# Low-rank latents: squares, sums and roots among the last projection panels, scaling and splitting in single steps beside neighbourhood heads

## The chip, the core and the metric

The kernel runs on one core of one Trainium2 chip. The metric is the device time of one execution, in microseconds (us), as the median of the runs shown. A core has TensorE (PE in the profile, with its weight loads as PEld), VectorE (DVE), ScalarE (ACT), GpSimd (POOL) and the DMA queue of SyncE (SP); each works through its own instructions in order, and semaphores hold an instruction until what it reads is there and what it overwrites has been read.

## What is computed

Two layers of a transformer over 512 latent tokens (on a grid 64 wide) and 256 context tokens, model width 1024. The first layer has two groups of heads, 8 heads of neighbourhood attention and 8 heads of multi-head latent attention (MLA), then SwiGLU; the second has sliding-window attention and SwiGLU. The change is in the MLA part of the first layer. There the input projection gives each token a query latent of 256 numbers and a key/value latent of 128, and each is normalised before it is used:

```python
def rms_norm(x, gain=None):
    y = xf * lax.rsqrt(jnp.mean(xf * xf, axis=-1, keepdims=True) + EPS)
    return y * gain
...
q = rms_norm(p[..., :MLA_Q_RANK], q_norm) @ w_q_up
c_kv = rms_norm(p[..., MLA_Q_RANK:MLA_Q_RANK + MLA_KV_RANK], kv_norm)
```

So each latent needs its squares, their sum over the features, a root with its reciprocal, and a multiplication by that factor and by the gain.

## The kernel before, in words

Activations lie with features on the 128 partitions and tokens along the free axis: 512 latent tokens (LATS), then 256 context tokens (CTXS). A product in full precision is three products of high and low parts: `mm3` issues wh x high (L335), wh x low (L337) and wl x high (L338) for each of 8 blocks of the contraction. High parts are ACT casts (L324 for weights, L361 in `split` for activations), low parts are differences on DVE (L325, L362).

The first layer begins with the modulated input (16 tiles) and then the loop `projections` (L1003): 12 panels of 128 weight columns, one after the other, each first for LATS and then for CTXS, each into a PSUM bank from a ring of seven (`PG`, L126). First come queries and keys of head pairs 0 and 1, then the panels that the string `AFTER` names in turn: 0, 1 and 2 are the query latent's two tiles and the key/value latent (tiles `lat_raw`, written by ACT at L738), k is the rotary key (rotated by ACT L464, DVE L465 and POOL L467 to L469), and 5 to 8 are queries and keys of head pairs 2 and 3. After each quarter of a panel the loop yields, and a share `DBG` of a modulation step is made beside it (`bg`). A modulation tile there is two halves of 512 columns: DVE multiplies and sums for one of the two condition vectors (L255, shown as ISA in the order and as CUSTOM_DVE in the profile, with L259 at the end), POOL multiplies in place for the other (L272), ACT sums (L273), DVE adds up (L275, L276).

Then come the neighbourhood heads, in pairs 0 to 3 (`na_jobs`, L1135). Each pair is three jobs: scores on PE (L745, L746) into three PSUM banks, a maximum on DVE that also frees the bank (`take`, L555), the exponential on ACT (L551), transposes on PE (L499) into banks that DVE (L490) or ACT (L491) copies out, products with the values (L545), at the end a factor for each query (L475 to L482). Beside each job `attend` lets a queue of side work advance by as many steps as `STEPS` says for that pair; a step is what a generator does up to its next yield. `ORDER` says what joins the queue at which pair: splitting of the raw queries and keys of pair 2 at pair 0, the latents' norms (n) and pair 3's splitting at pair 1, the preparation of the MLA heads (m) at pair 2.

The norms are `gained` (L968), called from `latent_norms` (L1050), in three steps. The first squares the three latent tiles on POOL (L978), adds the two squares of the query latent on DVE (L982), sums over the features on PE (L985: for each 128 tokens a product of the squares with one column of ones; twelve of them, in one bank), takes two roots on ACT (L988, behind a load of ACT's table for it) and the reciprocal on DVE (L989). The second and the third do one group each: for LATS and for CTXS PE spreads the factors over a bank (`spread`, L367; banks of the pair `PQ`, which the transposes of the heads use as well), DVE scales in place (L965), and ACT and DVE split into high and low parts (L361, L362).

The order in which instructions stand on each engine is decided by a scheduler that goes by the priorities of the program's text and by its own estimate of when each could run; it is fixed before the kernel runs.

Of the kernel before, what the change touches and what calls it, by code (L numbers as in the profile page):

```python
# [11 lines left out]
AF = mybir.ActivationFunctionType  # L12
ALU = mybir.AluOpType
# [39 lines left out]
OUTQ = 1  # L53
E1, EF = 1, 1
ORDER = ("2", "n3", "m", "")
AFTER = "012k5678"
DBG = 0.38
KC = (0, 1, 0)
VP = 0
TURN1, MANY = (0,), 0  # L60
# [8 lines left out]
PATTERN = ("fbsfbsfbbsfs",) * 3  # L69
BG = ((0, 0, 0, 0, 0), (2, 3), (0, 0), (0, 0))  # L70
FIRST = 2000
STEPS = ((2, 3, 4, 4), 5, 3)
HALVES = (slice(0, 256), slice(256, 512))
SWAP8 = [(i // 16) * 16 + (i % 16 + 8) % 16 for i in range(32)]
SWAP16 = [(i + 16) % 32 for i in range(32)]
# [23 lines left out]
def hybrid_kernel(ctx: ExitStack, tc, I, out):  # L99
# [17 lines left out]
    def B(dt=F32, tag="b"):  # L117
        return T(tag, [P, NT], dt)
# [226 lines left out]
    def PQ():  # L345
        return PS("d")
# [389 lines left out]
    def put(t, rows=P, scale=1.0):  # L736
        def use(src, c):
            marks["put"] = S.activation(t[:rows, c], src, AF.Copy, scale=scale)  # L738

        return use  # L740
# [216 lines left out]
    def gain(tiles, g0, col):  # L957

        for c in (LATS, CTXS):
            d, n = PQ(), c.stop - c.start  # L960
            for i in range(n // P):
                at = c.start // P + i
                spread(d[:, i * P : (i + 1) * P], col[:, at : at + 1].to_broadcast([P, P]))
            for j, t in enumerate(tiles):
                V.scalar_tensor_tensor(t[:, c], t[:, c], gains[:, g0 + j : g0 + j + 1], d[:, :n], op0=ALU.mult, op1=ALU.mult)  # L965
        return tiles

    def gained(groups):  # L968

        d, m = PQ(), NT // P  # L970
        n = m * len(groups)
        col = T("sm", [P, 6, 2]).rearrange("p a b -> p (a b)")[:, :n]
        for i, (tiles, _) in enumerate(groups):
            acc = None
            for t in tiles:
                s = B()
                if SQ:
                    G.tensor_tensor(s, t, t, op=ALU.mult)  # L978
                else:
                    S.activation(s, t, AF.Square)  # L980
                if acc is not None:
                    V.tensor_tensor(s, s, acc, op=ALU.add)  # L982
                acc = s
            for j in range(m):
                PE.matmul(d[:, i * m + j : i * m + j + 1], acc[:, j * P : (j + 1) * P], ones[:, :1], start=True, stop=True)  # L985
        for i, (tiles, _) in enumerate(groups):
            c = slice(i * m, i * m + m)
            S.activation(col[:, c], d[:, c], AF.Sqrt, bias=eps, scale=1.0 / (P * len(tiles)))  # L988
        V.reciprocal(col, col)  # L989
        yield  # L990
        for i, (tiles, g0) in enumerate(groups):
            res = [split(t, V) for t in gain(tiles, g0, col[:, i * m : i * m + m])]
            groups[i] = res
            yield

    rope0 = T("rope0", [P, 2, NL])
    behind(dma(rope0, I["rope0"]), marks["start"])
# [5 lines left out]
    def projections():  # L1003

        for p in range(2):
            yield from project(I["w_in0"][p], put_q(sets[p][0], 0.125), get=PG)
            yield from project(I["w_in0"][p + 4], put_k(sets[p][1], KC[0]), get=PG)
        for x in AFTER:
            if x in "012":
                lat_raw[int(x)] = B()  # L1010
                yield from project(I["w_in0"][8 + int(x)], put(lat_raw[int(x)]), get=PG)
            elif x == "k":
                kr.append(B())
                yield from project(I["w_kr"], put_rope(kr[0], rope0, SWAP8, 32, tag="p"), m=32, get=PG)
            else:
                raws.append(B(tag="p"))
                i = int(x) - 5
                yield from project(I["w_in0"][(2, 6, 3, 7)[i]], put(raws[i], scale=(0.125, 1.0)[i % 2]), get=PG)
# [774 lines left out]
```

## Time and profile before

| | |
|---|---|
| median of 3 runs | 1585.99 us (1585.27 to 1589.26) |
| the profiled execution, its own time | 1587.13 us |
| its span, first to last instruction | 1585.4 us |
| mean granted clock of PE | 0.994 |
| busy, of the span | PE 97%, DVE 73%, ACT 50%, POOL 19% |

The profile is of one execution. A line of the waits view names the engine and line that stood still, what it waited for, the sum, the number of times and the longest. A line of the timeline gives start and duration in us, engine, line, operation, what is written and read, and the shape. A line of a view by source line gives minimum, median and maximum duration in ns and the first and last start in us. A row of the windows view gives the busy time of each engine in a stretch and the clock that PE was granted, 1.00 being full speed. "x24" counts instructions; a product of plain 32-bit numbers, as L985, shows as two passes.

### The profile page before, as it was taken

The numbers are of one execution on the slowest core, as the hardware profiler recorded it, in microseconds if no ns is written. First come the engines' busy times: TensorE is split into PE (matmuls) and PEld (weight loads), VectorE is DVE, ScalarE is ACT, GpSimd is POOL, SyncE is SP. The second block draws the span as 40 slices with busy tenths as digits, with TensorE's granted clock in tenths as the row PEclk, the third lists the DMA queues.
The fourth block names the chain that finished last, engine by engine and source line by source line (L and its number), as shares of the span: only waits on it lengthen the run. The fifth ranks groups of instructions, "written<-read, shape, count | busy, mean of one in ns | idle before, by whom it ended". The sixth has DMA issues, their size and how long they took to land. (4 is left out here: it accounts for less than half of the span.)

```text
span 1585.4 us, 26553 instructions
## 1 busy us (share of the span) xinstructions
PE 1531.6 (97%) x10024; PEld 1375.6 (87%) x10024; DVE 1163.0 (73%) x2331; ACT 796.2 (50%) x1607; POOL 294.7 (19%) x316
## 2 busy tenths in 40 slices
PE   6999999999999999999999999989999999999998
PEld 4787778877998999998989998878889998899997
DVE  3885787676677696887768666868876778678685
ACT  4563687675555242332323334557756545454453
POOL 0144634210011101111020221492012000000001
PEclk9999999999999999999999998999999999999999
DMA  9745332004444645547475585131015123324222
GB/s 311 253 130 175 86 119 72 16 2 160 165 156 142 197 146 192 189 123 276 139 268 171 173 322 181 42 98 49 1 48 167 54 97 124 103 84 131 88 89 87
DMA packets 76464, 214.91 MB, mean 136 GB/s; under 512 B 9872, under 2 KB 16400, under 8 KB 76336
## 3 DMA queue, kind: packets, MB, share of 16 engines
q1 hardware_dynamic: 59216, 144.42, 28.2%
q0 software_dynamic: 15968, 67.24, 12.3%
q8 instruction: 78, 1.28, 0.3%
q10 hardware_dynamic: 1152, 1.57, 0.3%
q14 instruction: 50, 0.41, 0.1%
HBM read 186.97 MB, written 23.07 MB: 132 GB/s over the span
## 5 line engine op out<-in xcount | busy, mean ns | idle before, releaser
L324 ACT CAST wh<-wr 128x1024 fp32r<-128x1024 f32 (+2 forms) x148 | 115.4, 795 | 207.1 <-PE pss L1377 33.8
L325 DVE TENSOR_TENSOR wl<-wr,wh 128x1024 fp32r<-128x1024 f32 (+2 forms) x145 | 135.5, 942 | 79.8 <-ACT wh L324 79.6
L551 ACT ACTIVATE p<-p,sm 128x512 f32<-128x512 f32 (+3 forms) x144 | 104.9, 729 | 27.1 <-DVE sm L555 25.3
L233 DVE CUSTOM_DVE_ANT_0 p<-rope,cond 128x1024 bf16<-128x1024 f32 x64 | 77.1, 1221 | 47.5 <-DMA rope<-in_mod_w_dram 47.5
L1378 PE MATMUL pss<-b,wl 128*128 128x384 f32 (+1 forms) x346 | 106.9, 312 | 1.7 <-DVE wl L1364 1.7
L1376 PE MATMUL pss<-b,wh 128*128 128x384 f32 (+1 forms) x346 | 107.7, 312 | 0.6 <-ACT b L361 0.6
L1377 PE MATMUL pss<-b,wh 128*128 128x384 f32 (+1 forms) x346 | 107.9, 312 | 0.1
L337 PE MATMUL psd<-b,wh 128*128 128x512 f32 (+3 forms) x262 | 89.7, 342 | 0.0
L335 PE MATMUL psd<-b,wh 128*128 128x512 f32 (+3 forms) x222 | 80.1, 361 | 1.6 <-ACT b L464 1.2
L338 PE MATMUL psd<-b,wl 128*128 128x512 f32 (+3 forms) x222 | 78.5, 355 | 0.0
L545 PE MATMUL pso<-ph,b 128*64 128x256 f32 (+1 forms) x384 | 77.2, 359 | 0.4 <-DVE ph L490 0.4
L545 PE MATMUL pso<-pl,b 128*64 128x256 f32 (+1 forms) x384 | 76.7, 359 | 0.7 <-DVE pl L490 0.7
L1378 PE MATMUL pst<-b,wl 128*128 128x384 f32 (+1 forms) x226 | 70.8, 313 | 3.0 <-DVE wl L1364 3.0
L228 POOL DMA_DIRECT2D rope<-in_mod_w_dram x48 | 25.5, 532 | 244.0 <-DVE mod L233 230.9
L1377 PE MATMUL pst<-b,wh 128*128 128x384 f32 (+1 forms) x226 | 70.5, 312 | 0.0
L1376 PE MATMUL pst<-b,wh 128*128 128x384 f32 (+1 forms) x226 | 70.5, 312 | 0.0
L337 PE MATMUL pss<-b,wh 128*128 128x256 f32 (+3 forms) x216 | 69.6, 322 | 0.1
L1659 POOL TENSOR_TENSOR p<-p,p 128x256 f32<-128x256 f32 x6 | 4.6, 766 | 347.3 <-ACT p L1655 347.2
L335 PE MATMUL pss<-st,wh 128*128 128x512 f32 (+2 forms) x198 | 67.3, 340 | 1.1 <-ACT st L1168 0.8
L1378 PEld LDWEIGHTS pss<-b,wl 128*128 128x128 f32 x346 | 65.4, 190 | 2.5 <-DVE wl L1364 2.2
L338 PE MATMUL pss<-st,wl 128*128 128x512 f32 (+2 forms) x198 | 67.1, 339 | 0.0
L1376 PEld LDWEIGHTS pss<-b,wh 128*128 128x128 f32 x346 | 65.6, 190 | 1.1 <-ACT b L361 0.9
(623 smaller groups left out, 5403.9 us busy)
## 6 DMA issues: line engine op xcount, KB each, us to landing
wr<-in_w_gu_dram SPq DMA_DIRECT2D x88, 512.0 KB, 4.2
rope<-in_mod_w_dram POOLq DMA_DIRECT2D x48, 512.0 KB, 3.8
wr<-in_w_dn_dram SPq DMA_DIRECT2D x73, 256.0 KB, 2.9
wr<-in_w_out_dram SPq DMA_DIRECT2D x32, 512.0 KB, 3.5
p<-home POOLq DMA_DIRECT2D x40, 384.0 KB, 5.4
home<-p POOLq DMA_DIRECT2D x40, 384.0 KB, 4.9
wr<-in_w_in_dram SPq DMA_DIRECT2D x21, 512.0 KB, 4.6
nb<-in_nb_dram SPq DMA_DIRECT2D x16, 384.0 KB, 3.3
```

The lines of the kernel that those rows point to most:

```text
L228: G.dma_start(w, I["mod_w"][at])
L233: V.tensor_tensor_reduce(out=T("p", [P, D], mybir.dt.bfloat16), in0=w, in1=cond[:, v, :], op0=ALU.mult, op1=ALU.add, scale=1.0, scalar=0.0 ...
L324: behind(S.copy(h, r), *after[:1])
L325: behind((G if eng else V).tensor_tensor(lo, r, f(h), op=ALU.subtract), *after[1:])
L335: ins = PE.matmul(o, wh[:, k], mh[:, c], start=first and k == 0, stop=False)
L337: PE.matmul(o, wh[:, k], ml[:, c], start=False, stop=False)
L338: PE.matmul(o, wl[:, k], mh[:, c], start=False, stop=last and k == n - 1)
L545: ins = PE.matmul(o[64 * i : 64 * i + 64, c], v(kt), t, start=n == 0, stop=n == len(moving[i]) - 1)
L551: S.activation(p[:, c], p[:, c], AF.Exp, bias=nm, scale=-1.0, accum_out=dn)
L1376: PE.matmul(o, wh, xh, start=first and k == 0, stop=False, skip_group_check=not first)
L1377: PE.matmul(o, wh, xl, start=False, stop=False, skip_group_check=not first)
L1378: PE.matmul(o, wl, xh, start=False, stop=k == 3, skip_group_check=not first)
```

## The change

- The squares, sums, roots and reciprocals become a generator of their own, `latent_roots`, which the loop over projections runs as a step named r, behind the rotary key and ahead of panel 5. The squares go from POOL to ACT and into other buffers (p for b), the bank for the sums comes from the ring `PG`, and there is a reciprocal for each group.
- `gain` yields after LATS and after CTXS, and `gained` after the split of each tile: seven yields in place of two, and with the two steps of pair 3's splitting nine for that queue.
- The rate of side steps at pair 1 goes from 3 to 4 for each job; `DBG` goes from 0.38 to 0.375, since the loop has one yield more.

```diff
-AFTER = "012k5678"
-DBG = 0.38
+AFTER = "012kr5678"
+DBG = 0.375
...
-STEPS = ((2, 3, 4, 4), 5, 3)
+STEPS = ((2, 4, 4, 4), 5, 3)
...
                 V.scalar_tensor_tensor(t[:, c], t[:, c], gains[:, g0 + j : g0 + j + 1], d[:, :n], op0=ALU.mult, op1=ALU.mult)
-        return tiles
-
-    def gained(groups):
-
-        d, m = PQ(), NT // P
-        n = m * len(groups)
-        col = T("sm", [P, 6, 2]).rearrange("p a b -> p (a b)")[:, :n]
-        for i, (tiles, _) in enumerate(groups):
+            yield
+
+    roots = []
+
+    def latent_roots():
+
+        d, m = PG(), NT // P
+        groups = (lat_raw[2:], lat_raw[:2])
+        col = T("sm", [P, 6, 2]).rearrange("p a b -> p (a b)")[:, : m * len(groups)]
+        for i, tiles in enumerate(groups):
             acc = None
             for t in tiles:
-                s = B()
-                if SQ:
-                    G.tensor_tensor(s, t, t, op=ALU.mult)
-                else:
-                    S.activation(s, t, AF.Square)
+                s = B(tag="p")
+                S.activation(s, t, AF.Square)
                 if acc is not None:
                     V.tensor_tensor(s, s, acc, op=ALU.add)
                 acc = s
             for j in range(m):
                 PE.matmul(d[:, i * m + j : i * m + j + 1], acc[:, j * P : (j + 1) * P], ones[:, :1], start=True, stop=True)
-        for i, (tiles, _) in enumerate(groups):
+        for i, tiles in enumerate(groups):
             c = slice(i * m, i * m + m)
             S.activation(col[:, c], d[:, c], AF.Sqrt, bias=eps, scale=1.0 / (P * len(tiles)))
-        V.reciprocal(col, col)
+            V.reciprocal(col[:, c], col[:, c])
+            roots.append(col[:, c])
         yield
+
+    def gained(groups):
+
         for i, (tiles, g0) in enumerate(groups):
-            res = [split(t, V) for t in gain(tiles, g0, col[:, i * m : i * m + m])]
+            yield from gain(tiles, g0, roots[i])
+            res = []
+            for t in tiles:
+                res.append(split(t, V))
+                yield
             groups[i] = res
-            yield
...
+            elif x == "r":
+                yield from latent_roots()
```

In the changed kernel the squares are L979, the addition L981, the sums L984, the roots L987 and the reciprocals L988; lines further down have numbers 8 higher.

What the scheduler makes of it, at three places. PE in panel 5 (q of head pair 2), at the end of its latent columns, before; wh and wl are the panel's weights, b the input's tiles, and the bank (pst) is the panel's:

```order
L335 MATMUL pst_1485<-b_110,wh_1481 128x512
L337 MATMUL pst_1485<-b_111,wh_1481 128x512
L338 MATMUL pst_1485<-b_110,wl_1482 128x512
L335 MATMUL pst_1485<-b_112,wh_1481 128x512
L337 MATMUL pst_1485<-b_113,wh_1481 128x512
L338 MATMUL pst_1485<-b_112,wl_1482 128x512
L335 MATMUL pss_1520<-b_98,wh_1481 128x256
```

The same place on PE in the changed kernel; p_1480 is the square of the key/value latent, p_1490 the sum of the two squares of the query latent:

```order
L335 MATMUL pss_1510<-b_110,wh_1506 128x512
L337 MATMUL pss_1510<-b_111,wh_1506 128x512
L338 MATMUL pss_1510<-b_110,wl_1507 128x512
L984 MATMUL pst_1478<-ones_93,p_1480 128x1 x6
L984 MATMUL pst_1478<-ones_93,p_1490 128x1 x6
L335 MATMUL pss_1510<-b_112,wh_1506 128x512
L337 MATMUL pss_1510<-b_113,wh_1506 128x512
L338 MATMUL pss_1510<-b_112,wl_1507 128x512
L335 MATMUL psd_1545<-b_98,wh_1506 128x256
```

All twelve sums now stand in one piece ahead of the panel's last three products; before, they stood among the scores and transposes of head pair 1 in pieces of five, four and three.

DVE at that time, before: the second half of a modulation product, then the low part of the weights of panel 6 (wl), then small steps of the modulation:

```order
L255 ISA p_1504,mod_293_1376<-pl_1502,cond_66,mod_293_1376 128x512
L255 ISA mod_293_1376 128x1
L325 TENSOR_TENSOR wl_1651<-wr_1648,wh_1650 128x1024
L259 SCALAR_TENSOR_TENSOR mod_293_1376<-mod_293_1376,modb_89 128x1
L275 TENSOR_TENSOR mod_294_1377<-part_1469,part_1472 128x1
L276 SCALAR_TENSOR_TENSOR mod_294_1377<-mod_294_1377,modb_89 128x1
```

And DVE in the changed kernel, with the same modulation tile ahead:

```order
L255 ISA p_1529,mod_293_1376<-pl_1527,cond_66,mod_293_1376 128x512
L255 ISA mod_293_1376 128x1
L259 SCALAR_TENSOR_TENSOR mod_293_1376<-mod_293_1376,modb_89 128x1
L981 TENSOR_TENSOR p_1490<-p_1490,p_1488 128x768
L325 TENSOR_TENSOR wl_1676<-wr_1673,wh_1675 128x1024
L275 TENSOR_TENSOR mod_294_1377<-part_1469,part_1472 128x1
L276 SCALAR_TENSOR_TENSOR mod_294_1377<-mod_294_1377,modb_89 128x1
L988 RECIPROCAL sm_1479<-sm_1479 128x6 x2
```

The addition stands behind the modulation product and its last step, ahead of the weights' low part; the reciprocals come three instructions later.

DVE beside head pair 1, where the latents are scaled, before; b_1270 is the key/value latent, b_1068 and b_1153 are the query latent's tiles, psd the spread factors:

```order
L362 TENSOR_TENSOR b_2102<-b_1270,b_2101 128x768
L965 SCALAR_TENSOR_TENSOR b_1068<-b_1068,mla_gain_690,psd_2105 128x512
L965 SCALAR_TENSOR_TENSOR b_1153<-b_1153,mla_gain_690,psd_2105 128x512
L965 SCALAR_TENSOR_TENSOR b_1068<-b_1068,mla_gain_690,psd_2112 128x256
L965 SCALAR_TENSOR_TENSOR b_1153<-b_1153,mla_gain_690,psd_2112 128x256
L555 ISA p_2302,sm_2292<-pss_2301,zeros_95 128x256
```

The nearest group of them in the changed kernel, which stands earlier in the queue:

```order
L965 SCALAR_TENSOR_TENSOR b_1270<-b_1270,mla_gain_690,psd_2087 128x256
L965 SCALAR_TENSOR_TENSOR b_1068<-b_1068,mla_gain_690,psd_2106 128x512
L965 SCALAR_TENSOR_TENSOR b_1153<-b_1153,mla_gain_690,psd_2106 128x512
L490 COPY ph_2133<-pst_2128 128x512
L362 TENSOR_TENSOR b_2103<-b_1270,b_2102 128x768
L555 ISA wr_2163,sm_2024<-pss_2158,nb_2029 128x512
```

The scaling of the query latent is cut in two, with three maxima and a copy between its latent columns (shown) and its context columns (further down), and the split of the key/value latent now follows the first part.

## The prediction

> **What bounds the kernel now.** I read the page first, for the engine that is full:
>
> ```profile
> span 1585.4 us, 26553 instructions
> PE 1531.6 (97%) x10024; PEld 1375.6 (87%) x10024; DVE 1163.0 (73%) x2331; ACT 796.2 (50%) x1607; POOL 294.7 (19%) x316
> ```
>
> TensorE (PE) is busy for 1531.6 of 1585.4 us, so PE sets the time: work moved on another engine is worth what PE waits for it, and no more. The change touches two stretches, so next I cut them out with the windows view (columns: stretch, its length, then busy us of PE, PEld, DVE, ACT, POOL, each with a count, granted PE clock, DMA share, GB/s):
>
> ```profile
> 150.00:170.00 20.00, 20.00 (x118) 17.74 (x117) 18.85 (x33) 8.75 (x22) 13.92 (x10) 1.00 0.21 63
> 210.00:220.00 10.00, 8.00 (x59) 6.35 (x59) 8.85 (x21) 9.26 (x23) 5.00 (x6) 1.00 0.30 94
> ```
>
> Among the last projection panels (150 to 170 us) PE never stops, ACT has room (8.75 of 20) and DVE has almost none (18.85 of 20). Beside the first neighbourhood heads (they begin at 176 us) DVE and ACT are both near full (8.85 and 9.26 of 10) and PE has holes. How big the holes are, the waits of PE say, first from 176 to 195 us, then from 195 to 260 us, which is where the moved work lies now (us in total, times, longest):
>
> ```profile
> PE pss L745 <- DVE sm L555: 2.6, 4, 0.9
> ...
> PE psd L499 <- DVE b L965: 1.5, 1, 1.5
> PE pss L745 <- DVE sm L555: 0.5, 1, 0.5
> PE pst L499 <- DVE pl L490: 0.3, 1, 0.3
> PE psd L755 <- DVE b L490: 0.3, 1, 0.3
> PE psd L499 <- ACT b L464: 0.2, 1, 0.2
> PE pso L545 <- DVE ph L490: 0.2, 1, 0.2
> ```
>
> The second group adds up to 3.0 us. That is all that the change can win where its work lies now, 0.19% of the time; 0.3% (4.8 us) is about what a measurement of this kernel can tell from no change, and the three runs shown already lie 4.0 us apart.
>
> **Part 1: the sums of squares go into a PE stream without holes.** The twelve one-column sums stay the same PE work. They take
>
> ```profile
> 197.02 1.17 PE L985 MATMUL psd<-ones,b 128*128 128x1 f32 x10
> ```
>
> 1.17 us for ten passes, 24 passes in all (each of the twelve is two), so 0.11 us each and 2.7 us together: minus 2.7 us among the heads, plus 2.7 us among the panels, net 0. What matters is when they can start. In the new order all twelve stand together on PE, ahead of the last three matmuls of panel 5's latent columns (q of head pair 2). Its first matmul and the first of its last three, the panel's context columns and the next panel begin now as follows (start us, us); behind them an ACT cast with the 2.02 us that ACT idles ahead of it, the casts of 768 columns and the table load:
>
> ```profile
> 142.97 0.40 PE L335 MATMUL pst<-b,wh 128*128 128x512 f32 x1
> 147.76 0.39 PE L335 MATMUL pst<-b,wh 128*128 128x512 f32 x1
> 148.44 0.28 PE L335 MATMUL pss<-b,wh 128*128 128x256 f32 x1
> 151.31 0.40 PE L335 MATMUL psd<-b,wh 128*128 128x512 f32 x1
> ...
> 143.06 1.05 ACT L324 CAST wh<-wr 128x1024 fp32r<-128x1024 f32 x1 [2.02 <-PE psd L337]
> L361 ACT CAST b<-b x4: 823/830/834, 207.6 to 218.2; 128x768 fp32r<-128x768 f32 x3, 32x768 fp32r<-32x768 f32 x1
> L988 ACT ACT_TABLE_LOAD  x1: 1283/1283/1283, 201.8 to 201.8; - x1
> ```
>
> So PE reaches the sums at 147.8 us. The first six need one ACT square (0.83 us, as a cast of that size), and ACT is idle from 141.0 on: they run, 12 passes, until 149.1. The other six need the DVE addition of two squares (now L982, new L981), and DVE executes it behind two products for the modulation (L255) and a one-column step (L259). DVE and POOL at that place now:
>
> ```profile
> 142.40 2.90 DVE L255 CUSTOM_DVE_ANT_0 p<-pl,cond,mod 128x512 bf16<-128x512 f32 x1
> 148.18 0.15 DVE L259 SCALAR_TENSOR_TENSOR mod<-mod,modb 128x1 f32<-128x1 f32 x1
> 148.29 0.75 DVE L255 CUSTOM_DVE_ANT_0 p<-pl,cond,mod 128x512 bf16<-128x512 f32 x1
> 148.97 2.31 DVE L325 TENSOR_TENSOR wl<-wr,wh 128x1024 fp32r<-128x1024 f32 x1
> 151.20 1.26 DVE L259 SCALAR_TENSOR_TENSOR mod<-mod,modb 128x1 f32<-128x1 f32 x1
> ...
> 148.39 1.80 POOL L272 TENSOR_TENSOR ph<-ph,cond 128x512 f32<-128x512 f32 x1 [0.69 <-issue]
> 150.16 2.28 POOL L469 TENSOR_TENSOR b<-p,p 32x512 f32<-32x512 f32 x1
> 152.41 1.28 POOL L272 TENSOR_TENSOR pl<-pl,cond 128x512 f32<-128x512 f32 x1
> ...
> L982 DVE TENSOR_TENSOR b<-b,b 128x768 f32<-128x768 f32 x1 | 0.9, 947 | 0.0
> ```
>
> The same L255 takes 0.75 us at one place and 2.90 at another, and a one-column L259 takes 1.26 us: they end when a POOL operation ends (150.16, then 152.41), in turn with it. So DVE is free for the new queue at 149.0; L259 comes first and waits for POOL's L272, until 150.2, and takes 0.15 at its shortest. Then either the addition runs at once (0.95 us, done at 151.3) or POOL's L469, which stands ready, goes first for its own 1.1 us (2.28 less the 1.12 us that it waited for L325), and the addition is done at 152.4. If nothing blocked DVE at all it would be done at 150.1. PE's wait from 149.1 is therefore 1.0, 2.2 or 3.3 us; I take 3.0, near the upper end, because L325 and L259 in the rows above took turns with POOL in just that way.
>
> Behind the waiting sums stand, on PE, the rest of that panel and everything after it; on ACT, the table load (1.28 us) and the two roots, and behind them the next panels' casts; on DVE, the two reciprocals (0.2 us each) and the next low parts. None of that is late next: the low part of the next panel follows the addition directly (2.3 us in the row above) and is needed only after 2.7 us of sums, 0.7 us and a panel half of 2.9 us. The three squares on ACT (2.5 us) fill the 2.0 us of idle time and push the cast back by 0.5 us, 7 us before PE begins the panel that needs it: 0.
>
> **Part 2: the clock.** From 147.8 to about 153.5 PE would do nothing but one-column passes and wait, 1.3 + 3.0 + 1.3 = 5.6 us. What such a stretch does to the granted clock:
>
> ```profile
> 177.37:180.78 3.41, 1.81 (x9) 1.10 (x9) 3.35 (x11) 2.79 (x8) 3.25 (x3) 1.00 0.46 115
> 180.78:184.20 3.42, 3.42 (x18) 3.42 (x18) 1.11 (x6) 2.96 (x10) 3.26 (x3) 0.50 0.40 82
> 979.50:982.92 3.42, 3.42 (x18) 3.42 (x18) 0.04 (x1) 0.23 (x1) 0.00 (x0) 0.50 0.04 11
> L387 PE MATMUL pss<-ones,p x32: 250/352/353, 978.7 to 984.5; 128*128 128x1 f32 x32
> ```
>
> Half busy for 3.4 us (1.81 of 3.41) and the clock was 0.50 for the next 3.4 us; at 979.5 us PE is shown busy, with one-column sums (L387), and the clock was 0.50 as well. So I expect one or two stretches of 3.4 us at half clock here: six sums at half speed cost 1.0 us more (12 passes, 0.19 us each at 979 us instead of 0.11), and some 2 us of the panels at half speed 1.0 more. I take 2.0; the ends are 0 and 3.4 (two whole stretches, 6.8 us, at half). The Trainium skill (TensorE: Matmul & The Clock Gate, What's actually happening) halves the clock only after an idle window of about 3.4 us. By that rule a wait of 3.0 us leaves the clock alone, and this term is 0 instead of 2.0. The trace differs: in the first row above no single wait was longer than 0.9 us, and the clock fell all the same.
>
> **Part 3: what the heads get back.** Out of the stretch from 195 to 215 us go two loads of ACT tables (one only moves, the reload for the exponential goes altogether), two roots and a reciprocal, for which DVE waited 1.8 us:
>
> ```profile
> L989 DVE RECIPROCAL sm<-sm 128x12 f32<-128x12 f32 x1 | 0.2, 227 | 1.8 <-ACT sm L988 1.8
> L965 DVE SCALAR_TENSOR_TENSOR b<-b,mla_gain,psd 128x512 f32<-128x512 f32 x3 | 2.1, 743 | 0.0
> L965 DVE SCALAR_TENSOR_TENSOR b<-b,mla_gain,psd 128x256 f32<-128x256 f32 x3 | 1.3, 476 | 0.0
> 199.07 0.69 DVE L490 COPY pl<-pst 128x512 f32<-128x512 f32 x1
> 209.99 0.95 DVE L362 TENSOR_TENSOR b<-b,b 128x768 fp32r<-128x768 f32 x1
> 210.86 2.19 DVE L965 SCALAR_TENSOR_TENSOR b<-b,mla_gain,psd 128x512 f32<-128x512 f32 x4
> ```
>
> The largest hole of PE, 1.5 us, has a cause in the last two rows: four scalings and a split, 3.1 us, in which DVE frees no bank for PE. In single steps that block is gone, but the new order has another: a short scaling, two long ones, a copy of transposed tiles and a split, with no maximum (L555) among them, 0.48 + 1.48 + 0.69 + 0.95 = 3.6 us. DVE comes to it with the 1.8 us in hand. I take half of the 3.0 us back: minus 1.5; ends minus 3.0 (all gone) and plus 1.5 (the new block costs what the old one did, on top).
>
> From 184.8 to 189.1 us POOL squares the latents now, three times 1.47 us, and a one-column DVE step waits for it:
>
> ```profile
> L978 POOL TENSOR_TENSOR b<-b x3: 1468/1469/1471, 184.8 to 187.6; 128x768 f32<-128x768 f32 x3
> 188.02 1.11 DVE L276 SCALAR_TENSOR_TENSOR mod<-mod,modb 128x1 f32<-128x1 f32 x1
> ```
>
> Without the squares L276 takes 0.15, and 0.95 us of DVE's lag goes where PE waits for L555: minus 0.5, ends minus 1.2 and 0. The other waits from 176 to 184 us stay: their DVE order doesn't change.
>
> Later the scheduler has shifted single instructions up to the second layer, and one more PSUM bank is drawn from the ring. Nothing in the trace favours a side: 0, ends plus and minus 1.5. The new rates of steps (4 for 3) and of modulations (0.375 for 0.38) leave the number of both the same: 0.
>
> **The sum.** 3.0 + 2.0 - 1.5 - 0.5 = plus 3.0 us on the profiled execution's 1587.13 us, that is 1590.1. That execution lies 1.1 us above the median of the runs (1585.99), so I predict 1589.0, 0.19% above the median: not to be told from no change.
>
> **The rivals.**
> - *The clock holds.* The wait comes, but without half clock: plus 1.0, 1587.0. For it: after the waits of 1.5 us at 209 to 213 us the clock stayed at 1.00. Against it: the two rows at 0.50. Chance 0.17. (It is the case of the rule on idle windows in the Trainium skill, TensorE: Matmul & The Clock Gate, What's actually happening.)
> - *The wait does not come.* If DVE is early by 2 us (POOL's products fall elsewhere), the addition is there at 149.1 and only part 3 remains: minus 2.0, and up to minus 5.9 if all of the 3.0 and 1.2 us go and the half clock at 180.78 (1.7 us) with them. The middle is 1582.0. Against it: POOL's order is the same up to that place. Chance 0.20; more than half of it (0.12) beyond 0.3%.
> - *The clock makes it slower.* If the low stretch fills two clock windows, the gate stays at half for 6.8 us, 3.4 us lost, with a wait of 3.3; and if the heads' new block of 3.6 us eats its gain (0 for minus 1.5 and 0.5), the sum is plus 6.7, 1592.7. It decides from a wait of about 2.2 us on, since then 1.3 + 2.2 + 1.3 us hold more than one window of 3.4. Chance 0.18.
> - *Forecast*: wait and one window's worth at half clock, 1589.0: 0.45.
>
> Range 1582.0 to 1593.0: it leaves out the far half of the second rival (about 0.12) and the tail of the third (about 0.07). Faster by over 0.3% (below 1581.2): 0.12. Slower by over 0.3% (above 1590.8): the third rival and 0.05 of the forecast, 0.23. Within: 0.65.
>
> **What would show it.** In the waits of PE between 140 and 160 us: a wait for the DVE addition (L981) of 2 to 3.4 us; none or under 1 us, and part 1 is wrong. In the windows there: a clock of 0.50 for 3.4 us or more. Between 195 and 260 us: waits of about 1.5 us in place of 3.0, none for L965 longer than 1 us. The ACT rows: one table load for the roots before 160 us and none between 195 and 215. If the span falls by more than 4 us, parts 1 and 2 are wrong; if it grows by more than 5, part 3 is.

## The result, and the profile after

The changed kernel takes 1597.07 us (median of 7 runs, 1592.33 to 1600.97), the kernel before beside it 1585.99 us (7 runs, 1581.54 to 1589.53). The ratio is 1.0059, with a 95% interval of 1.0043 to 1.0075: slower by more than 0.3%, and above the predicted range (the two medians by themselves give 1.0070, inside that interval). The profiled execution took 1597.83 us, 10.7 us more than that of before (1587.13). First its page:

```profile
span 1596.1 us, 26546 instructions
PE 1536.9 (96%) x10024; PEld 1380.7 (87%) x10024; DVE 1164.6 (73%) x2332; ACT 796.1 (50%) x1609; POOL 290.0 (18%) x313
```

The number of PE's instructions is the same, yet PE is busy for 5.3 us longer (1536.9 for 1531.6): a part of the loss is clock, and the rest is waiting. To see where, I compare how far PE has come. The windows view counts PE's instructions in a stretch; here are the stretches from the start that hold the first 750, 1250, 1500 and 2000, for the kernel before and then for the changed one (the second column is the time that it took):

```profile
0.00:137.48 137.48, 122.69 (x750) 96.64 (x751) 90.19 (x196) 68.97 (x147) 30.93 (x26) 1.00 0.70 238
0.00:218.79 218.79, 198.77 (x1250) 160.45 (x1251) 154.74 (x333) 120.80 (x270) 76.60 (x59) 0.99 0.56 185
0.00:252.80 252.80, 231.81 (x1500) 187.55 (x1500) 182.32 (x396) 145.83 (x329) 89.31 (x68) 0.99 0.53 172
0.00:320.47 320.47, 299.47 (x2000) 242.93 (x2001) 228.40 (x536) 195.14 (x441) 113.08 (x86) 0.99 0.45 144
```

```profile
0.00:136.07 136.07, 120.56 (x750) 95.31 (x751) 90.69 (x194) 68.86 (x147) 30.92 (x26) 0.99 0.71 241
0.00:220.36 220.36, 199.91 (x1251) 162.53 (x1253) 151.72 (x330) 118.18 (x263) 70.60 (x55) 0.96 0.55 182
0.00:262.60 262.60, 236.31 (x1501) 193.31 (x1501) 184.03 (x398) 146.16 (x331) 86.28 (x66) 0.95 0.51 166
0.00:329.80 329.80, 303.25 (x2001) 248.26 (x2001) 230.93 (x537) 195.44 (x444) 109.41 (x83) 0.96 0.43 140
```

The changed kernel is 1.4 us ahead at the 750th instruction, before anything was changed (the clock and the loads of the start differ from one execution to the next), 1.6 us behind at the 1250th, 9.8 at the 1500th, 9.3 at the 2000th and 10.7 at the end. So, in this pair of executions, about 3.0 us go in the stretch of the panels and the first heads, and 8.2 us between the 1250th and the 1500th instruction, that is from 220 to 263 us, beside the later heads. Nothing that counts is lost after that.

**The first 3.0 us: the sums among the panels.** The sums and what they waited for, on PE, DVE and POOL:

```profile
146.17 1.39 PE L984 MATMUL pst<-ones,p 128*128 128x1 f32 x12
149.51 2.72 PE L984 MATMUL pst<-ones,p 128*128 128x1 f32 x12 [1.95 <-DVE p L981]
...
147.50 1.09 DVE L259 SCALAR_TENSOR_TENSOR mod<-mod,modb 128x1 f32<-128x1 f32 x1
148.51 0.95 DVE L981 TENSOR_TENSOR p<-p,p 128x768 f32<-128x768 f32 x1
...
146.80 1.77 POOL L272 TENSOR_TENSOR ph<-ph,cond 128x512 f32<-128x512 f32 x1 [0.69 <-issue]
148.54 2.06 POOL L469 TENSOR_TENSOR b<-p,p 32x512 f32<-32x512 f32 x1
```

It went as the prediction had it in its middle case: L259 ended with POOL's L272 (148.57), the addition went next, L469 after it. PE waited for 1.95 us. Its second half took 2.72 us where the first took 1.39, and the clock shows why:

```profile
145.21:148.63 3.42, 2.35 (x17) 2.07 (x16) 3.38 (x7) 1.15 (x5) 2.73 (x3) 1.00 0.40 111
148.63:152.05 3.42, 2.54 (x12) 2.54 (x13) 3.42 (x3) 1.98 (x3) 3.42 (x2) 0.50 0.36 121
152.05:155.46 3.41, 3.41 (x14) 3.12 (x15) 3.38 (x10) 1.75 (x5) 2.32 (x2) 0.50 0.23 65
...
150.00:170.00 20.00, 20.00 (x106) 17.99 (x107) 15.81 (x33) 8.58 (x22) 12.05 (x9) 0.86 0.18 53
```

Two windows of 3.41 us at half clock, up to 3.4 us lost. In the last row, which answers to that of before, PE is busy all the time as it was, but with 106 matmuls in place of 118.

The first heads lose clock too. In the kernel before, one window beside them was at half (180.78 us, in the prediction); here two are, one after the other, which is up to 1.7 us more:

```profile
182.75:186.17 3.42, 2.40 (x12) 1.40 (x10) 3.33 (x8) 3.09 (x8) 3.22 (x4) 1.00 0.54 132
186.17:189.58 3.41, 3.09 (x15) 3.09 (x15) 1.65 (x8) 2.47 (x8) 3.25 (x3) 0.50 0.27 58
189.58:193.00 3.42, 3.42 (x17) 3.42 (x17) 0.34 (x1) 0.76 (x4) 1.05 (x1) 0.50 0.39 115
```

Against this stands what was won before the 1250th instruction: in the kernel before, PE waited there 0.55 us at 209.51 us (L555) and 1.54 us at 212.41 us (L965), and the changed kernel has neither wait.

**The next 8.2 us: DVE stands still among the heads.** The row for 210 to 220 us looks like a success: PE is full, where it had been busy for 8.00 us. The waits of PE from 195 to 262 us, below, have no L965 any more either. But three others have come: 2.8 us at 227.06 us (L482), 1.3 us at 245.52 us (L555; the other 1.4 us of that line lie at 199.74 us) and 1.7 us at 247.74 us (L490, where 0.3 us stood before). They fill most of two clock windows, and the window behind each is at half:

```profile
210.00:220.00 10.00, 10.00 (x82) 7.50 (x78) 9.80 (x23) 8.21 (x21) 0.00 (x0) 1.00 0.47 158
223.72:227.13 3.41, 0.61 (x4) 0.17 (x3) 3.35 (x4) 1.80 (x6) 2.42 (x2) 1.00 0.50 154
227.13:230.55 3.42, 3.42 (x16) 3.24 (x16) 3.02 (x9) 1.62 (x4) 0.00 (x0) 0.50 0.00 0
244.19:247.61 3.42, 0.54 (x3) 0.30 (x2) 3.34 (x8) 0.86 (x3) 2.40 (x2) 1.00 0.00 0
247.61:251.03 3.42, 3.29 (x15) 3.29 (x16) 1.84 (x8) 1.44 (x5) 0.00 (x0) 0.50 0.00 0
```

```profile
PE pst L499 <- DVE b L482: 2.8, 1, 2.8
PE pss L745 <- DVE sm L555: 2.7, 2, 1.4
PE psd L755 <- DVE b L490: 1.7, 1, 1.7
```

From 223.72 to 227.13 us PE works for 0.61 us, while DVE shows 3.35 us of work. Its instructions, POOL's beside them, and then a second place of the same kind, DVE first and POOL behind:

```profile
221.85 3.17 DVE L362 TENSOR_TENSOR b<-b,b 32x768 fp32r<-32x768 f32 x1
225.05 1.51 DVE L1113 CAST st<-b 32x768 fp32r<-32x768 f32 x1
226.59 0.42 DVE L482 TENSOR_TENSOR b<-b,pst 128x256 f32<-128x256 f32 x1
...
221.82 4.32 POOL L325 TENSOR_TENSOR wl<-wr,wh 128x1024 fp32r<-128x1024 f32 x2 [18.85 <-ACT wh L324]
...
242.03 2.97 DVE L1113 CAST st<-b 32x768 fp32r<-32x768 f32 x1
245.03 0.42 DVE L555 CUSTOM_DVE_ANT_0 p<-pss,zeros 128x256 f32<-128x256 f32 x1
245.50 1.58 DVE L1113 CAST st<-b 32x768 fp32r<-32x768 f32 x1
...
241.40 1.84 POOL L1117 TENSOR_TENSOR st<-b,st 64x768 fp32r<-64x768 f32 x1 [6.10 <-ACT st L1116]
243.18 1.40 POOL L1110 MEMSET st<- 32x768 f32 x2
```

L362 is here the low part of the rotary key (32 partitions), the first work of MLA's preparation (`mla_prepare`, beside pair 2); L1113 copies it into the operands of the heads. POOL's row of 4.32 us is two instructions, the low parts of the MLA weights w_ukv and w_qr, in one piece. DVE's 0.94 us of work takes 3.17, its copy of 0.55 us takes 1.51; and behind them on DVE stands the last product of pair 1 (L482), which frees the bank that PE's transposes wait for. The four copies in the kernel before, by line, and then in the changed one:

```profile
L1105 DVE CAST st<-b 32x768 fp32r<-32x768 f32 x4 | 4.1, 1040 | 0.1
```

```profile
L1113 DVE CAST st<-b 32x768 fp32r<-32x768 f32 x4 | 6.6, 1654 | 0.1
```

With the split, five operations take 9.8 us in place of 5.0. The Trainium skill (Trainium Architecture — The Big Picture, What this means for kernel authors) has it that of the engines only DVE and GpSimd contend for SBUF, and as an exclusive lock, not a shared bandwidth. The trace agrees: 3.17 us beside the POOL pair, 0.94 us without it.

In the kernel before, the timeline of POOL and DVE there has both low parts ended (219.65 + 1.28 = 220.93) when the key's split begins:

```profile
212.08 2.38 POOL L325 TENSOR_TENSOR wl<-wr,wh 128x1024 fp32r<-128x1024 f32 x1 [18.90 <-ACT wh L324]
219.65 1.28 POOL L325 TENSOR_TENSOR wl<-wr,wh 128x512 fp32r<-128x512 f32 x1 [2.80 <-ACT wh L324]
...
221.42 0.94 DVE L362 TENSOR_TENSOR b<-b,b 32x768 fp32r<-32x768 f32 x1
...
235.76 2.98 DVE L1105 CAST st<-b 32x768 fp32r<-32x768 f32 x2
```

The two places must be kept apart. The first meeting, with the weights' low parts, is missing in the kernel before. The second is there as well: its last row is the second pair of copies, 2.98 us for two, beside POOL's L1109 (235.43 us) and MEMSET (237.18 us), and only 0.3 us of PE's waits follow. So of the 5.8 us of new waits 2.8 belong to the meeting that the change made, and 3.0 to one that was there already and held PE up for 0.3 us.

What brought the low parts and the split together stands in ACT's order, since POOL's low part follows ACT's cast of the weight. Before, ACT cast w_ukv (the first row) well ahead of the rotary key, at 210.92 and 218.17 us in the profile:

```
L324 CAST wh_2327<-wr_2325 128x1024
...
L361 CAST b_2343<-b_1388 32x768
L324 CAST wh_2333<-wr_2331 128x512
```

In the changed kernel the key comes first, and both weights right behind it:

```
L361 CAST b_2344<-b_1388 32x768
L324 CAST wh_2328<-wr_2326 128x1024
L491 COPY pl_2317<-psd_2312 128x512
L324 CAST wh_2334<-wr_2332 128x512
```

No line of the diff speaks of these operations. Their new order is the scheduler's: the program's text, by whose priorities it goes, moved with the steps and the sums.

### The profile page after: what moved, and what is told of

Its sections match the earlier page's. It is cut to its first block, busy times and chain, and to the rows that moved or that the text cites. A ratio compares the mean times of both kernels' runs of the same rounds, so it can differ in the third digit from the quotient of the medians.

```text
span 1596.1 us, 26546 instructions
## 1 busy us (share of the span) xinstructions
PE 1536.9 (96%) x10024; PEld 1380.7 (87%) x10024; DVE 1164.6 (73%) x2332; ACT 796.1 (50%) x1609; POOL 290.0 (18%) x313
## 3 DMA queue, kind: packets, MB, share of 16 engines
q8 instruction: 78, 1.28, 0.3%
## 5 line engine op out<-in xcount | busy, mean ns | idle before, releaser
L325 DVE TENSOR_TENSOR wl<-wr,wh 128x1024 fp32r<-128x1024 f32 (+2 forms) x145 | 135.2, 940 | 82.7 <-ACT wh L324 81.8
L1386 PE MATMUL pss<-b,wl 128*128 128x384 f32 (+1 forms) x304 | 94.7, 311 | 1.7 <-DVE wl L1372 1.6
L1384 PE MATMUL pss<-b,wh 128*128 128x384 f32 (+1 forms) x304 | 94.3, 310 | 0.0
L1385 PE MATMUL pss<-b,wh 128*128 128x384 f32 (+1 forms) x304 | 94.2, 310 | 0.0
L337 PE MATMUL pss<-b,wh 128*128 128x256 f32 (+3 forms) x250 | 81.5, 328 | 3.4 <-DVE b L424 1.7
L337 PE MATMUL psd<-b,wh 128*128 128x512 f32 (+3 forms) x244 | 82.2, 337 | 0.0
L335 PE MATMUL psd<-b,wh 128*128 128x512 f32 (+3 forms) x220 | 77.4, 352 | 1.0 <-ACT b L464 0.7
L335 PE MATMUL pss<-st,wh 128*128 128x256 f32 (+2 forms) x230 | 76.9, 335 | 0.6 <-ACT st L1371 0.6
L338 PE MATMUL pss<-st,wl 128*128 128x256 f32 (+2 forms) x230 | 76.8, 334 | 0.0
L1385 PE MATMUL psd<-b,wh 128*128 128x384 f32 (+1 forms) x234 | 72.4, 309 | 0.0
L1384 PE MATMUL psd<-b,wh 128*128 128x384 f32 (+1 forms) x234 | 72.3, 309 | 0.0
L1386 PE MATMUL psd<-b,wl 128*128 128x384 f32 (+1 forms) x234 | 72.0, 309 | 0.0
L745 PE MATMUL pss<-st,st 128*128 128x256 f32 (+3 forms) x194 | 61.8, 339 | 4.6 <-DVE sm L555 4.3
L499 PE MATMUL pst<-ident_r,p 128*128 128x128 f32 x346 | 62.2, 283 | 4.0 <-DVE b L482 2.8
```

What stands on the lines that cost most here:

```text
L325: behind((G if eng else V).tensor_tensor(lo, r, f(h), op=ALU.subtract), *after[1:])
L335: ins = PE.matmul(o, wh[:, k], mh[:, c], start=first and k == 0, stop=False)
L337: PE.matmul(o, wh[:, k], ml[:, c], start=False, stop=False)
L338: PE.matmul(o, wl[:, k], mh[:, c], start=False, stop=last and k == n - 1)
L745: PE.matmul(o, x, ks[0][:, keys], start=True, stop=False)
L1384: PE.matmul(o, wh, xh, start=first and k == 0, stop=False, skip_group_check=not first)
```

## The experiments

All times are medians of the runs beside runs of the kernel before on the same chip; the ratio is to that kernel, with its 95% interval. Theory A: the loss is the sums' new place (wait and clock) and, apart from it, DVE standing still beside POOL among the heads. Its rivals: only the sums' place costs (B); the single steps cost (C); the bank drawn from the ring (D); ACT's squares and separate roots (E).

**The parts alone.** `roots_only` takes the sums among the panels, with scaling and splitting in two coarse steps at the old rate:

```diff
-STEPS = ((2, 4, 4, 4), 5, 3)
+STEPS = ((2, 3, 4, 4), 5, 3)
...
-            yield from gain(tiles, g0, roots[i])
-            res = []
-            for t in tiles:
-                res.append(split(t, V))
-                yield
-            groups[i] = res
+            gain(tiles, g0, roots[i])
+            groups[i] = [split(t, V) for t in tiles]
+            yield
```

> Squares, sums, roots and reciprocals among the panels as in the changed kernel; scaling and splitting in two coarse steps and the rate 3 as before. Theory A (DVE and POOL in turn among the heads): the wait for the addition of about 2 us and two half-clock windows come at 147 to 156 us (plus 3 to 5 us), but the heads from 195 to 260 us are as before, because the weights' casts no longer fall together with the split of the rotary key: no PE wait above 1.5 us there, time 1588 to 1591. Theory B (the sums' new place is what costs): as the whole change, 1595 to 1598. Theory C (the fine steps cost by themselves): at most 1589.

Measured: 1590.22 us, 1.0028 (1.0014 to 1.0042). The wait for the addition is 2.0 us again, two windows are at half clock from 147.82 us, and from 195 to 262 us the waits sum to 3.3 us, 1.3 the longest. As A has it; the sums' place costs 4 to 5 us. Among the heads nothing more is lost: from PE's 1250th to its 1500th instruction it takes 34.1 us, and 34.0 in the kernel before.

`steps_only` is the other part: the kernel before with the yields in `gain` and `gained` and the rate 4; squares on POOL, sums and roots beside pair 1.

> Squares on POOL, sums and roots beside head pair 1 as before; only the scaling and splitting in single steps and the rate 4. Theory A: what costs is the place where the two weights' low parts on POOL meet the rotary key's split on DVE, and here the split stands behind them: no PE wait above 1.5 us between 195 and 260 us, time 1584 to 1589. Theory B: no sums among the panels, so as before, 1584 to 1588. Theory C (the fine steps cost by themselves): PE waits of 5 us or more from 195 to 260 us, time 1591 to 1595.

Measured: 1578.10 us, 0.9946 (0.9928 to 0.9965), and once more in more rounds:

> The steps alone once more, in more rounds. If the gain is of the order of the steps and not of windows that happened to fall well in four runs: 1576 to 1581. Else 1582 to 1586.

Measured: 1578.29 us, 0.9964 (0.9947 to 0.9980). So the steps by themselves gain 0.36 to 0.54%, 6 to 9 us, and C falls, as long as the sums stand where they stood. The windows of the kernel before, and of the steps alone (first run):

```profile
195.00:262.00 67.00, 63.83 (x497) 52.39 (x494) 53.04 (x130) 52.83 (x127) 25.09 (x22) 1.00 0.36 109
```

```profile
195.00:262.00 67.00, 66.97 (x525) 55.82 (x522) 57.61 (x145) 55.18 (x135) 24.91 (x22) 1.00 0.37 112
```

PE is busy for 66.97 of 67 us, and issues 28 matmuls more: the 3.0 us that the prediction gave as the most that could be won there were won in full, and this is the version that beats both kernels. Its four copies and its split of the rotary key take 2.7 + 1.2 us. Neither of the two edits does it alone:

> The kernel before with the rate 4 at pair 1 and nothing else. If the rate is what gains in the steps alone: 1577 to 1581 and no PE wait from 195 to 262 us. If the single steps are: 1583 to 1588, the wait of 1.5 us for the scaling (L965) still there.

> The steps alone with the rate left at 3. If the single steps are what gains: 1577 to 1581, no wait for the scaling (L965) above 0.5 us. If the rate is: 1583 to 1588.

Measured: the rate alone 1584.40 us, 0.9988 (0.9972 to 1.0004), the waits for L965 (1.8 us) still there; single steps at the old rate 1586.65 us, 1.0007 (0.9985 to 1.0029), with 2.3 us of waits for a copy of ACT, 1.5 for one of DVE and 0.7 still for L965. So each run rules its own edit out as the whole cause: the gain takes both.

**The bank.** `ring` is the kernel before with `ring = [1]` in place of `[0]`:

> The kernel before, with the ring of banks begun one bank later, and nothing else. Theory A: the order of single instructions moves, the time moves by what falls together among the heads, between 1583 and 1590. Theory D (the extra bank drawn from the ring is the cause, by the shifted banks): 1593 to 1598.

Measured: 1585.99 us, 1.0000 (0.9987 to 1.0014). D falls.

**DVE and POOL.** `kr_off` takes the rotary key from DVE, in the changed kernel:

```diff
-        KR.extend(split(kr[0][:32, :NT], V))
+        KR.extend(split(kr[0][:32, :NT], G))
...
-                    V.tensor_copy(KA[s][i][ROPE[s]], KR[i][:32])
+                    S.copy(KA[s][i][ROPE[s]], KR[i][:32])
```

> The changed kernel, with the rotary key's low part made on POOL in place of DVE and its four copies into the key operands on ACT in place of DVE. Theory A: the PE waits of 2.8 us at 227 us and of 1.3 and 1.7 us at 245 to 248 us go, with the half-clock windows behind two of them: 5 to 9 us less than the changed kernel, 1588 to 1592. Theory B: they are a consequence of where the sums stand, or of banks, and stay: 1595 to 1598.

Measured: 1591.42 us, 1.0033 (1.0016 to 1.0051), 5.7 us below the changed kernel by the medians and 4.1 by the ratios. The wait of 2.8 us is gone, and of 7.2 us of waits from 195 to 262 us 3.5 are left. The same edit in the kernel before is the control:

> The kernel before with the rotary key's low part on POOL and its copies on ACT. Theory A: the same time as before within 0.2%, 1583 to 1588, since the split doesn't meet the weights' low parts there. Theory H (less DVE work helps wherever it is): 1577 to 1581.

Measured: 1586.10 us, 1.0007 (0.9989 to 1.0025): no gain where the split meets no work of POOL. And in the steps alone:

> The steps alone (sums beside head pair 1, squares on POOL) with the rotary key's low part on POOL and its copies on ACT. Theory A: nothing fell together there, so nothing to gain: within 0.2% of the steps alone, 1575 to 1581. Theory H (less DVE work helps wherever it is): 1570 to 1575.

Measured: 1581.22 us, 0.9991 (0.9973 to 1.0009). No gain either; most of the steps' gain is gone (PE now waits 2.0 us for one of ACT's copies), against A's expectation of no difference.

These still left open whether DVE stood still or had too much to do. `low_on_dve` gives DVE more work, the two weights' low parts, and takes them from POOL; DVE's order is otherwise that of the changed kernel up to the second pair of copies, which here stand back to back, without the maximum between them:

```diff
-        wu["kv"] = load_w(I["w_ukv"], 2, 512, G)
-        w = load_w(I["w_qr"], 2, 256, G)
+        wu["kv"] = load_w(I["w_ukv"], 2, 512)
+        w = load_w(I["w_qr"], 2, 256)
```

> The changed kernel with the low parts of two MLA weights (w_ukv 128x1024, w_qr 128x512) made on DVE in place of POOL: DVE has two operations more, in an order that is otherwise the same, and POOL has none beside the rotary key's split. Theory A (DVE stands still while POOL's pair runs): the split takes about 1 us in place of 3.2, its first copy about 0.6 in place of 1.5, the PE wait of 2.8 us is under 1.5: 2 to 6 us less than the changed kernel, 1591 to 1595. Theory H (DVE has too much to do there): two more operations make it worse, 1598 to 1602.

Measured: 1590.35 us, 1.0032 (1.0018 to 1.0046), 6.7 us below the changed kernel by the medians and 4.3 by the ratios. The intervals of the ratios overlap by a little, for `kr_off` too; of the ten runs here two (1592.46 and 1592.48 us) lie above the fastest of the changed kernel (1592.33). The split and its first copy on DVE:

```profile
217.98 0.94 DVE L362 TENSOR_TENSOR b<-b,b 32x768 fp32r<-32x768 f32 x1
218.95 0.55 DVE L1113 CAST st<-b 32x768 fp32r<-32x768 f32 x1
```

0.94 and 0.55 us where they took 3.17 and 1.51, in a DVE with more to do. That DVE stood still at the first meeting is shown by this. The second is untouched: its two copies take 3.69 us here beside POOL's L1117 and MEMSET, and PE waits 2.9 us for the maximum (L555) behind them. Whether the rate brings the two together, `rate3` tells, the changed kernel with the 3 of before in `STEPS`:

> The changed kernel with the rate left at 3, so that nine steps fill nine places. If the rate 4 brings the weights' low parts beside the rotary key's split: the waits from 225 to 250 us fall under 2 us and the time to 1588 to 1592. If the early sums do it, whatever the rate: 1595 to 1599.

Measured: 1599.61 us, 1.0094 (1.0066 to 1.0123). Not the rate: with the sums among the panels the heads lose at either rate, here by a wait of 3.1 us for ACT's rotary copy (L464) and 3.4 us for L555. The split takes 0.94 us in this kernel, with none of POOL's low parts beside it. So the meeting explains what the changed kernel loses, but not all that early sums and single steps can lose together.

**The place of the sums.** `no_add` leaves the addition out and lets PE add the squares in the bank:

```diff
-                if acc is not None:
-                    V.tensor_tensor(s, s, acc, op=ALU.add)
-                acc = s
+                sq.append(s)
...
-                PE.matmul(d[:, i * m + j : i * m + j + 1], acc[:, j * P : (j + 1) * P], ones[:, :1], start=True, stop=True)
+                for k, s in enumerate(sq):
+                    PE.matmul(d[:, i * m + j : i * m + j + 1], s[:, j * P : (j + 1) * P], ones[:, :1], start=k == 0, stop=k == len(sq) - 1)
```

> The changed kernel without the DVE addition: PE adds the two squares of the query latent in the bank, six more one-column products (12 passes, 1.3 us). Theory A: the wait of 2.0 us behind DVE goes, one or two half-clock windows with it, the heads stay as in the changed kernel: 2 to 5 us less than it, 1592 to 1595. Theory F (the clock falls for one-column passes, not for the wait): the half-clock windows at 148 to 156 us stay, gain at most 1 us, 1596 to 1598.

Measured: 1590.35 us, 1.0024 (1.0007 to 1.0040). PE has no wait from 130 to 176 us, and the clock falls all the same. The sums on PE and three windows:

```profile
145.88 5.55 PE L983 MATMUL pst<-ones,p 128*128 128x1 f32 x36
```

```profile
144.80:148.21 3.41, 3.41 (x28) 3.22 (x26) 3.38 (x6) 1.26 (x4) 2.71 (x2) 1.00 0.32 103
148.21:151.62 3.41, 3.41 (x17) 3.41 (x17) 3.38 (x4) 0.72 (x2) 3.41 (x3) 0.50 0.41 135
151.62:155.04 3.42, 3.42 (x14) 3.13 (x14) 1.39 (x7) 2.91 (x6) 0.20 (x1) 0.50 0.21 77
```

A window in which PE shows no idle time, 2.3 us of it one-column products, is followed by half clock. F's cause holds for the clock, and A's, that half clock goes with the wait, fails; F's time (a gain of 1 us at most) doesn't hold, since the wait did cost and the heads lost a little less (5.3 us of waits from 195 to 262 us in place of 7.2).

`sums_apart` issues the twelve in six pieces of two, six products between pieces: `latent_roots` yields after the squares and after each second product, and the loop over the panels behind takes one step of it beside each of its own (`DBG` is back at 0.38):

```diff
-                    yield from project(I["w_in0"][(2, 6, 3, 7)[i]], put(raws[i], scale=(0.125, 1.0)[i % 2]), get=PG)
+                for _ in project(I["w_in0"][(2, 6, 3, 7)[i]], put(raws[i], scale=(0.125, 1.0)[i % 2]), get=PG):
+                    next(sums, None)
+                    yield
```

> The changed kernel, with the twelve one-column sums issued in six pieces of two, six products of panels 5 and 6 between pieces, squares and addition where they were. Theory A (place of the sums, in one piece, and separately what falls together among the heads): no PE wait above 0.5 us and no half-clock window from 130 to 176 us, the waits from 225 to 250 us stay: 4 to 7 us less than the changed kernel, 1590 to 1593. Theory G (the heads are late only because PE and the side work came late from the panels): the waits from 225 to 250 us go as well, 1578 to 1584.

Measured: 1595.14 us, 1.0082 (1.0051 to 1.0113), not to be told from the changed kernel. The panels did as expected (clock 1.00, no wait), and the heads took it back: the same wait of 2.8 us, the split at 3.1 us, and half clock at 221 us.

```profile
148.00:160.00 12.00, 12.00 (x79) 10.90 (x79) 11.37 (x19) 5.11 (x14) 9.13 (x5) 1.00 0.34 111
221.12:224.53 3.41, 2.40 (x11) 2.22 (x11) 3.31 (x9) 0.60 (x2) 0.09 (x1) 0.50 0.00 0
```

With both repairs:

> Both repairs in the changed kernel: sums in six pieces, and the rotary key's low part on POOL and its copies on ACT. Theory A: both losses go, what is left are waits of about 3.5 us among the heads as before: 1583 to 1587. If single steps gain whatever else stands there, as they did alone: 1576 to 1581.

Measured: 1587.07 us, 1.0022 (1.0006 to 1.0038), with 2.3 us of waits left from 195 to 262 us: what A said to 0.1 us, though the interval leaves 1 out, and the gain of the steps isn't there. Last, `late_act`, the whole change but for the place of the sums:

```diff
-AFTER = "012kr5678"
-DBG = 0.375
+AFTER = "012k5678"
+DBG = 0.38
...
-        d, m = PG(), NT // P
+        d, m = PQ(), NT // P
...
+        yield from latent_roots()
         yield from gained(groups)
```

> The whole change but for the place of the sums: squares on ACT into the other buffers, two reciprocals, single steps, rate 4, and squares, sums and roots beside head pair 1 as before. Theory A (place of the sums and what then falls together among the heads): as with the steps alone, no PE wait above 1 us from 195 to 262 us, 1576 to 1582. Theory E (the squares on ACT and the separate roots cost, wherever they stand): 1585 or more.

Measured: 1584.65 us, 1.0002 (0.9985 to 1.0018): neither loss nor gain, which fits neither A (1576 to 1582) nor, by 0.4 us, E. Without the sums among the panels none of the loss is left: it hangs on their place, directly and by what it does to the order. That the gain is missing has its cause in the squares, as the steps alone with ACT's squares (`SQ` 0 for 1) show:

> The steps alone, with the squares on ACT in place of POOL, same buffers. If the squares on ACT are what took away the gain when all but the place of the sums was changed (1584.7 against 1578.1): 1583 to 1587. If it was the other buffers, the reciprocal for each group or half-clock windows that fell by chance: 1576 to 1581.

Measured: 1586.39 us, 1.0005 (0.9986 to 1.0023): squares on ACT beside the heads cost what the steps gain (E, for that place). From 176 to 262 us PE waits 5.8 us there for the maxima (L555).

Taken together: the sums among the panels with coarse steps cost 0.28% (`roots_only`), the single steps on top of them bring it to 0.59%, and `kr_off` and `low_on_dve`, which end the first meeting, bring it back to 0.33 and 0.32%. The loss among the heads needs both edits at once.

## Why the prediction was wrong

- **Part 1, the wait**: right. It gave 1.0, 2.2 or 3.3 us and took 3.0; it was 1.95. PE reached the sums 1.6 us earlier than thought. One reading in it is loose: of the two ends of POOL's work that it names, no DVE operation shown ends at 150.16 us; L325 began its own work there.
- **Part 2, the clock**: the mechanism right, the size at the upper end: two windows (up to 3.4 us) in place of the 2.0 us taken, and a further one beside the first heads (up to 1.7 us), which the sum did not have. The point from which the third rival was to decide, a wait of 2.2 us, was wrong: `no_add` has two windows without any wait. The rule on an idle window that the rival "the clock holds" rested on (the Trainium skill, TensorE: Matmul & The Clock Gate, What's actually happening) fails here again: behind 182.75 us the clock is halved, though PE was busy for 2.40 of 3.42 us and no wait there is longer than 0.85 us. That the windows run freely, which the same section says, agrees with the trace: they are 3.41 us long and begin anywhere.
- **Part 3, the heads**: the step that failed. It took minus 1.5 and minus 0.5 and bounded the loss at plus 1.5; PE lost 8.2 us there. What it named did come: L965 keeps PE waiting no longer, the load for the roots is at 149 us and the reload behind it is gone, and L276 takes 0.16 us. The minus 0.5 itself did not come: in front of the same product of PE where it waited 0.77 us (192.33 us) it now waits 1.40 us (199.74 us), because DVE, rid of the squares, stands there for 2.22 us until a DMA (tile nb) has landed. And it priced only the moved operations and the new block next to them. It left out that the steps behind in the same queue, MLA's preparation, move against the engines that do not step with them: the cast of w_ukv went from ahead of the rotary key to behind it, POOL's two low parts came to stand beside DVE's split, and PE paid 2.8 us of waits for it, 3.0 more at the second pair of copies, and up to 3.4 us of clock for both. The prediction had this very turn-taking in its part 1, with a row for it, and did not look for it a second time.
- **"The new rates leave the number of both the same: 0"** failed too: the number is the same, the place is not. With the steps alone that place is worth 6 to 9 us. In its two profiles PE is 6.3 and 3.6 us ahead at the 2000th instruction; the first is rid of the half clock at 180.78 us as well as of the 3.0 us of waits.
- **Later reorder, 0 within 1.5**: right; from the 2000th instruction to the end the difference grew by 1.4 us.
- **The rivals**: the third (two windows, and the heads give nothing) was the nearest, at 1592.7; it lacked the meeting of DVE and POOL. The second rival's chances don't fit its own sums: spread evenly from 1580.1 to 1584.0, less than half of it lies below 1581.2, not more than half. "If it grows by more than 5, part 3 is wrong" is what happened.

Not settled: why the scheduler, with the sums among the panels and single steps, sets these casts so late; it decides by its own estimate, which no run here shows. Nor is it settled why `rate3` loses as much without the meeting. How the 8.2 us divide between waits and half clock isn't settled either, since the two hang together.

## What to carry to other kernels

When a change moves steps of a queue, compare the order of everything behind them in that queue, on every engine that shares a path, and look for the pairs that were seen to block each other: the cost came from operations that no line of the diff names. A handful of tiny products in one piece is not cheap by its duration alone: spread them between long ones, which kept the clock here, though the heads took the gain back. And compare waits by the instruction behind them, not by the clock on the wall: the heads begin some 6 us later in the changed kernel, so a fixed stretch of time holds other work. And try the parts of a change alone: the steps alone gain 0.4 to 0.5%, while the whole lost 0.6%.

## What the hardware showed that was not expected

- A DVE cast with one input (32x768, 0.55 us by itself) takes 1.51 to 2.97 us beside POOL, so it is not only operations that read two tiles that stand still. What this costs depends on what stands behind: two such copies take 4.00 us in `roots_only`, where no wait of PE from 195 to 262 us is longer than 1.3 us.
- Half clock follows one-column products even where PE shows no idle time (three windows of `no_add` above).
- Nearly the same waits (2.7 to 2.9 us in all) cost up to 3.4 us, up to 1.7 us (the kernel before) or nothing of clock, by how they fall into the windows. The steps alone were profiled twice: from 176 to 195 us PE is busy for 16.01 us at clock 1.00 in one, and 15.88 us at 0.82 in the other:

```profile
176.00:195.00 19.00, 16.01 (x117) 12.46 (x117) 15.81 (x42) 16.48 (x39) 17.02 (x12) 1.00 0.48 135
```

```profile
176.00:195.00 19.00, 15.88 (x90) 13.18 (x89) 11.88 (x35) 13.73 (x33) 16.29 (x11) 0.82 0.43 112
```
